# Six Strassen blocks in two runs of three instead of seven in one run, one weight sum of each made a block ahead by an adding DMA

## The chip, the cores and the metric

The kernel runs on one core of a Trainium2 chip. The metric is the device time of one execution in microseconds. Before the change it is 1360.77 us, the median of three runs (1360.38 to 1362.2). A core has five engines with a queue of their own: TensorE (PE) does matrix products, VectorE (DVE) and ScalarE (ACT) work on tiles in on-chip memory, GpSimd (POOL) does small work and issues the DMAs that add while they write, SyncE (SP) issues most plain DMAs. Each engine takes its instructions in program order and waits on semaphores.

## The reference

Two layers on a sequence of 512 tokens of width 1024. Layer 0 mixes by retention and neighbourhood attention, layer 1 by a state space scan. After each mixer stands the same channel mixer, in which most of the change lies:

```python
def conv_geglu_ffn(hn, w_up, conv_w, conv_b, w_down):
    u = depthwise_conv_centered(hn @ w_up, conv_w, conv_b)
    gate, val = jnp.split(u, 2, axis=-1)
    return (jax.nn.gelu(gate, approximate=True) * val) @ w_down
```

`w_up` has 2 x 2816 columns: 22 feature blocks of 128 columns for the gate and 22 for the value, f = 0 to 21.

## The kernel before

**Products.** Every float32 product is made of three TensorE products in a faster format: an operand x is split into a high part (a cast on ACT, L115) and a low part (x minus the high part, on DVE, L116), and `mm3` adds high by high, low by high and high by low (L125, L126, L127). So every 128 x 1024 weight tile costs ACT one cast and DVE one subtraction before TensorE can use it. The split weights go into a ring of four places (`weight`), each free again when TensorE has used it; the loaded tiles before that stand in a pool of three (`wst`).

**Up-projection.** `ffn` takes the blocks f one after another. A plain block needs 24 products of 512 columns for the gate and 24 for the value, then its `tail`: the convolution (three instructions for each of gate and value, two of them on DVE), gelu, and the product into `H[:, f]`.

**Strassen blocks.** For f in `UP` the pair f, f + 1, gate and value together, is one 2 x 2 block product by Winograd's form of Strassen's rule: seven products in place of eight, each of 24 matmuls of 256 columns, 168 matmuls in all (`up_strassen`). The combinations of the activations are made once (`combos`). Those of the weights are made in each block by `weights(i)` just before product i: four tiles are loaded, q11, q12, q22 and q21 (`w_up[s, f + h]`); DVE makes q12 + q22, then q0 = q11 + (q12 + q22), later q0 + q21 (three additions, L469); and one more sum, q11 + `w_up[1, f]`, is made by a DMA that adds (L484, issued by POOL). The seven tiles are split like any others. DVE also adds three of the results into G and V, and the `tail`s of the pair are done during the next block (`held`). With `UP = (6, 8, 10, 12, 14, 16, 18)` seven such blocks follow each other without a break; f = 20, 21 are plain again.

**Tiles that stay.** q11, q12 and so on live in the three `wst` tiles and two `gain` tiles that `E.held` keeps for a whole run of blocks; block number `nth` takes them by `(2 * nth + j) % 3`.

**Order.** The program is written in order of dependence; the scheduler of the recording layer then puts each engine's instructions in order by priority, and an instruction of low priority whose inputs are ready may move forward. `weights(i)` stands in `tc.high_priority(60)`. The first step of the down-projection's preparation, `A21 = A11 - A21` over H[:, :11] (L329 in `raw`), moves forward this way as soon as the blocks f = 0 to 10 are done: it then stands on DVE inside a Strassen block. `E.in_turn` orders the instructions of a block after the last split and load.

**Chores.** The down-projection also uses combinations of its weights. They are sums in DRAM, 32 DMAs of 704 KB a layer issued by POOL (L293 in `sums`): 16 copies and 16 that add. `E.chore()` issues the next one, after the last product that has been recorded. They are called in the mixer of the same layer (a "c" in the strings `PAIRS` and `SLOTS` that order the steps of a head pair or group), after plain blocks, and twice in each Strassen block (i = 1 and 4).

**State space layer.** `SLOTS` has one string for each of four groups: h = one head (its rows `pb` are loaded by ACT's queue, three buffers ahead), i and p = parts of a pair's output, n = a projection of the next group, o = an output projection, c = a chore.

Of the kernel before, what the change touches and what calls it, by code (L numbers as in the profile page):

```python
# [8 lines left out]
F32 = mybir.dt.float32  # L9
# [4 lines left out]
ALU = mybir.AluOpType  # L14
# [3 lines left out]
P = 128  # L18
# [382 lines left out]
    E.late += [lambda s=s: E.finish(s, st, done) for s in LATE]  # L401


UP = (6, 8, 10, 12, 14, 16, 18)


def combos(E, pool, raw):
# [38 lines left out]
def up_strassen(E, pool, w_up, f, X, G, V, held):  # L446

    nc, tc = E.nc, E.tc  # L450
    low, high = slice(0, HW), slice(HW, S)

    nth = UP.index(f)
    if f - 2 not in UP:
        E.held = [[E.wst.tile([P, 1024], F32, name="wst") for _ in range(3)],
                  [E.gain.tile([P, D], F32, name="gain") for _ in range(2)]]
    (st12, st11), (st0, st21) = [E.held[0][(2 * nth + j) % 3] for j in range(2)], E.held[1]

    def load(st, s, h):
        E.load = nc.sync.dma_start(st, w_up[s, f + h])  # L460
        return st

    def parts(st, i):
        hi, lo = E.weight(SKEW if i else 0)
        E.split(hi, lo, st)
        E.last = E.pair + (E.load,)
        return hi, lo

    add = lambda o, x, y: nc.vector.tensor_tensor(o, x, y, op=ALU.add)  # L469
    q = {}  # L470

    def weights(i):
        with tc.high_priority(60), E.in_turn():
            if i == 0:
                q[11] = load(st11, 0, 0)
                return parts(q[11], i)
            if i == 1:
                q[12] = load(st12, 1, 0)
                with E.in_turn(E.load):
                    q[22] = load(pool.tile([P, 1024], F32, name="wu", tag=f"e{nth % 2}"), 1, 1)  # L480
                add(q[12], q[12], q[22])
                q[0] = st0
                add(q[0], q[11], q[12])
                nc.gpsimd.dma_start(q[11], w_up[1, f], accum_op=ALU.add, max_dma_last_dim=4096)  # L484
                return parts(q[12], i)
            if i == 2:
                return parts(q[0], i)
            if i == 3:
                q[21] = load(st21, 0, 1)
                add(q[0], q[0], q[21])  # L490
                return parts(q[0], i)
            return parts(q[{4: 11, 5: 21, 6: 22}[i]], i)

    a = E.mm.tile([P, S], F32, name="mm")
    b, d = (E.px.tile([P, S], F32, name="pu", tag="px") for _ in range(2))
    order = ("A11", a), ("S3", b), ("S2", a), ("A22", b), ("R1", a), ("A12", d), ("S4", a)
    for i, (n, bank) in enumerate(order):
        hi, lo = weights(i)
        more = i in (2, 3, 4, 6)
        r = bank.rearrange("p (j c) -> p j c", j=2)  # L500
        for j in range(2):
            for k in range(4):
                c = slice(j * 512 + k * P, j * 512 + k * P + P)
                E.mm3(r[:, j], hi[:, c], lo[:, c], X[n][0][:, k], X[n][1][:, k], not more and j + k == 0, k == 3, more or j > 0)
        if i in (3, 5):
            o = G[:, :, low if i == 3 else high]
            add(o, r, o)
        elif i == 4:
            t = E.tmp.tile([P, 2, HW], F32, name="w5", tag="tmp")
            nc.scalar.copy(t, r)  # L510
            add(V[:, :, low], t, V[:, :, low])
        else:
            nc.scalar.copy({0: G[:, :, high], 1: V[:, :, low], 2: G[:, :, low], 6: V[:, :, high]}[i], r)
        if i in (1, 4):
            E.chore()
        if i in (3, 5) and held:
            held.pop(0)()


def ffn(E, w_up, cw, w_down, ts, g_post_row, done, w1=None):  # L520
# [3 lines left out]
    with ExitStack() as ctx:  # L524
# [44 lines left out]
        for f in range(2, NF):  # L569
            if f in UP or f - 1 in UP:  # L570
                if f in UP:
                    G, V = (cp.tile([P, 2, S], F32, name=n, tag=t) for n, t in
                            ((("G", "k0"), ("V", "k1")) if UP.index(f) % 2 else (("G", "k2"), ("V", "k3"))))
                    up_strassen(E, hp, w_up, f, X, G, V, held)
                    held.extend(partial(tail, f + j, G[:, j], V[:, j], True) for j in range(2))
                    while held and f + 2 not in UP:
                        held.pop(0)()
                continue
            ps = []
            for s in range(2):  # L580
                behind = w1 and f == 2
                with E.in_turn() if f > UP[0] else nullcontext():
                    st = E.wload(w_up[s, f], E.mid if behind and s == 0 else None)
                    w = E.wunit(None, st=st, behind=E.turned[3][1] if behind else None)
                E.last = E.pair + (E.load,)
                ps.append(E.mm.tile([P, S], F32, name="mm"))
                E.proj_fm(ps[-1], w)
            tail(f, *ps)
            E.chore(1 + (f == 2))
            if f < UP[0]:  # L590
                X = next(make)
            if f == NF - 2:
                big = hp.tile([P, 32, HW], R32, name="big")
                for k in range(0, HK, 4):
                    c = slice(k, min(k + 4, HK))
                    E.split(big[:, c], big[:, HK + k:HK + c.stop], H[:, c, HW:])
# [40 lines left out]
def mixer0(E, w0, w_v, w_fm, tabs, dist_d, logit, gn, bias, w_out, g_post_row, done):  # L637
# [286 lines left out]

SLOTS = (
# [4 lines left out]
)  # L930

# [563 lines left out]
```

## Time and profile before

| What | Value |
| --- | --- |
| Time, median of three runs | 1360.77 us |
| Time of the profiled execution | 1356.96 us |
| Span of the profiled execution | 1355.2 us |
| TensorE busy | 1325.2 us (98%) |
| VectorE busy | 1124.9 us (83%) |
| ScalarE busy | 841.6 us (62%) |
| Seven Strassen blocks, layer 0 | 340.61 to 481.85 us |
| Seven Strassen blocks, layer 1 | 1083.43 to 1221.81 us |
| Groups 1 and 2 of the state space layer | about 774 to 923 us |

The profile names an instruction by engine, source line, operation and tiles (`out<-in`). A busy TensorE says little here, since the end of a matmul is modelled and overlaps the next one's start: the distance from one start to the next is its pace. A number in brackets at the end of a timeline row is the engine's idle time before that instruction and who ended it.

### The profile page before, as it was taken

The numbers are of one execution on the slowest core, as the hardware profiler recorded it, in microseconds if no ns is written. First come the engines' busy times: TensorE is split into PE (matmuls) and PEld (weight loads), VectorE is DVE, ScalarE is ACT, GpSimd is POOL, SyncE is SP. The second block draws the span as 40 slices with busy tenths as digits, with TensorE's granted clock in tenths as the row PEclk, the third lists the DMA queues.
The fourth block names the chain that finished last, engine by engine and source line by source line (L and its number), as shares of the span: only waits on it lengthen the run. The fifth ranks groups of instructions, "written<-read, shape, count | busy, mean of one in ns | idle before, by whom it ended". The sixth has DMA issues, their size and how long they took to land.

```text
span 1355.2 us, 20474 instructions
## 1 busy us (share of the span) xinstructions
PE 1325.2 (98%) x7784; PEld 1139.2 (84%) x7784; DVE 1124.9 (83%) x1554; ACT 841.6 (62%) x1353; POOL 125.5 (9%) x144
## 2 busy tenths in 40 slices
PE   7999999999999999999999999999999999999998
PEld 6877777898999988888778788787879899998886
DVE  7368888696799998797878876798789789999886
ACT  5356667453565766664878878477545467666663
POOL 1011111101110000020000110011011111110001
PEclk9999999999999999999999999999999999999999
DMA  8454447348983545564466475285544789684654
GB/s 294 146 208 161 159 135 217 103 123 197 217 206 100 151 143 194 190 210 129 138 181 195 126 247 185 90 250 162 183 133 152 203 197 220 166 225 146 193 183 148
DMA packets 71393, 237.28 MB, mean 175 GB/s; under 512 B 8576, under 2 KB 9344, under 8 KB 70784
## 3 DMA queue, kind: packets, MB, share of 16 engines
q1 hardware_dynamic: 54224, 167.30, 36.8%
q0 software_dynamic: 9184, 53.48, 17.6%
q10 hardware_dynamic: 7888, 15.21, 4.2%
q8 instruction: 61, 1.00, 0.3%
q14 instruction: 36, 0.29, 0.1%
HBM read 228.35 MB, written 51.64 MB: 207 GB/s over the span
## 4 chain that ended last, share of the span: by engine, by line
PE 77%; DVE 10%; ACT 5%; DMA 4%; issue 3%; SPq 1%; POOL 0%; DVEq 0%; POOLq 0%; ACTq 0%
PE mm L125 20%; PE mm L127 20%; PE mm L126 20%; DVE ring L116 3%; PE pu L126 2%; PE pu L125 2%; PE pu L127 2%; DMA pb<-pd 1%; PE pi L1155 1%; PE st L1104 1%; ACT pb L1134 1%; PE py L1175 1%; DVE cv L533 1%; DMA wst<-in_c_fm 1%; PE pt L182 1%
## 5 line engine op out<-in xcount | busy, mean ns | idle before, releaser
L125 PE MATMUL mm<-xh,ring 128*128 128x512 f32 (+1 forms) x880 | 321.0, 365 | 1.3 <-ACT z L1074 0.9
L116 DVE TENSOR_TENSOR ring<-wst,ring 128x1024 fp32r<-128x1024 f32 (+1 forms) x218 | 265.4, 1222 | 67.4 <-ACT ring L115 67.2
L127 PE MATMUL mm<-xl,ring 128*128 128x512 f32 (+2 forms) x880 | 320.0, 364 | 1.1 <-DVE mean L958 0.6
L126 PE MATMUL mm<-xh,ring 128*128 128x512 f32 (+2 forms) x880 | 319.8, 364 | 1.1 <-DVE ring L116 1.1
L115 ACT CAST ring<-wst 128x1024 fp32r<-128x1024 f32 (+1 forms) x218 | 224.4, 1034 | 122.3 <-PE mm L126 64.0
L125 PEld LDWEIGHTS mm<-xh,ring 128*128 128x128 f32 x880 | 165.4, 188 | 29.3 <-issue 2.7
L127 PEld LDWEIGHTS mm<-xl,ring 128*128 128x128 f32 (+1 forms) x880 | 165.1, 188 | 28.1 <-issue 1.1
L126 PEld LDWEIGHTS mm<-xh,ring 128*128 128x128 f32 (+1 forms) x880 | 165.4, 188 | 27.0 <-DVE ring L116 1.7
L125 PE MATMUL mm<-xc,ring 128*128 128x256 f32 x336 | 93.1, 277 | 0.0
L127 PE MATMUL mm<-xc,ring 128*128 128x256 f32 x336 | 93.1, 277 | 0.0
L126 PE MATMUL mm<-xc,ring 128*128 128x256 f32 x336 | 93.1, 277 | 0.0
L1134 ACT ACTIVATE pb<-pb,tok 128x128 f32<-128x128 f32 x256 | 80.7, 394 | 10.0 <-DMA pb<-pd 8.9
L125 PE MATMUL mm<-ring,big 128*128 128x512 f32 x164 | 64.0, 390 | 0.0
L127 PE MATMUL mm<-ring,big 128*128 128x512 f32 x164 | 63.8, 389 | 0.0
L126 PE MATMUL mm<-ring,big 128*128 128x512 f32 x164 | 63.8, 389 | 0.0
L127 PEld LDWEIGHTS mm<-xc,ring 128*128 128x128 f32 x336 | 63.1, 188 | 0.0
L125 PEld LDWEIGHTS mm<-xc,ring 128*128 128x128 f32 x336 | 63.1, 188 | 0.0
L126 PEld LDWEIGHTS mm<-xc,ring 128*128 128x128 f32 x336 | 63.0, 188 | 0.0
L125 PE MATMUL pu<-xh,ring 128*128 128x256 f32 x224 | 62.5, 279 | 0.1
L126 PE MATMUL pu<-xh,ring 128*128 128x256 f32 x224 | 62.3, 278 | 0.1
L127 PE MATMUL pu<-xl,ring 128*128 128x256 f32 x224 | 62.1, 277 | 0.0
L293 POOL DMA_DIRECT2D ts<-in_f_down x48 | 31.0, 652 | 280.3 <-PE mm L127 229.5
(360 smaller groups left out, 3120.8 us busy)
## 6 DMA issues: line engine op xcount, KB each, us to landing
ts<-in_f_down POOLq DMA_DIRECT2D x48, 704.0 KB, 6.3
wst<-in_f_up SPq DMA_DIRECT2D x60, 512.0 KB
wst<-in_c_fm SPq DMA_DIRECT2D x40, 512.0 KB
wst<-ts SPq DMA_DIRECT2D x32, 512.0 KB
pb<-pd ACTq DMA_DIRECT2D x29, 512.0 KB
wst<-in_f_down SPq DMA_DIRECT2D x24, 512.0 KB
ts<-ts POOLq DMA_DIRECT2D x16, 704.0 KB, 7.2
wst<-in_ab_fm SPq DMA_DIRECT2D x20, 512.0 KB
```

What stands on the lines that cost most here:

```text
L115: first = self.nc.scalar.copy(hi, src)
L116: second = self.nc.vector.tensor_tensor(lo, src, hi.bitcast(F32), op=ALU.subtract)
L125: mm(out, lh, rh, start=first, stop=False)
L126: mm(out, ll, rh, start=False, stop=False)
L127: self.product = mm(out, lh, rl, start=False, stop=last)
L182: last = nc.tensor.transpose(pt[:, j], xs[:, j * P:(j + 1) * P], self.ident)
L293: out.append(lambda i=i, src=src, j=j, c=c, kw=kw: gp.dma_start(part(ts, i, c), part(src, j, c), **kw))
L533: nc.vector.scalar_tensor_tensor(o[:, :S - 1], ps[:, 1:], w(2), o[:, :S - 1], op0=ALU.mult, op1=ALU.add)
L1104: nc.tensor.matmul(ps, o["bt"][:, c], xs, start=True, stop=True)
L1134: nc.scalar.activation(pb[:, dr, c], pb[:, dr, c], AF.Identity, scale=1.0 - 2 * dr, bias=tok[:, 0, c, dr * H + h:dr * H + h + 1])
L1155: nc.tensor.matmul(pi[:, c - 1 + dr], o["st"][dr, i][:, q * P:(q + 1) * P], o["t"][1][:, c * C:(c + 1) * C], start=True, stop=True)
L1175: E.together([nc.tensor.matmul(py[j * 64:j * 64 + 64, c * C:(c + 1) * C], o["x"][:, c, (2 * q + j) * 64:(2 * q + j + 1) * 64], ms[j][0][:, c],
```

## The change

- `UP` loses 12: f = 12 and 13 become plain blocks, so the Strassen blocks stand in two runs of three, f = 6, 8, 10 and f = 14, 16, 18.
- In the first block of a run all is as before. In the second and third, q12 + q22 is no longer made by DVE: during product 2 of the block before, SP loads the next block's q12 into the third kept tile (`ahead`) and POOL issues a DMA that adds q22 to it (`onto`). q22 itself, which the last product needs, is loaded at product 3 of its own block.
- Every load of a run is ordered after the load before it (`in_turn(E.load)`).
- `E.chore()` is called once in a Strassen block (i = 4) instead of twice.
- `SLOTS` gets four more "c": two in the string of group 1, two in that of group 2.

```diff
-UP = (6, 8, 10, 12, 14, 16, 18)
+UP = (6, 8, 10, 14, 16, 18)
...
-    (st12, st11), (st0, st21) = [E.held[0][(2 * nth + j) % 3] for j in range(2)], E.held[1]
-
-    def load(st, s, h):
-        E.load = nc.sync.dma_start(st, w_up[s, f + h])
+    first, more_blocks = f - 2 not in UP, f + 2 in UP
+    (st12, st11, ahead), (st0, st21) = [E.held[0][(2 * nth + j) % 3] for j in range(3)], E.held[1]
+
+    def load(st, s, h, f=f):
+        with E.in_turn(E.load):
+            E.load = nc.sync.dma_start(st, w_up[s, f + h])
         return st
+
+    def onto(st, f, h):
+        nc.gpsimd.dma_start(st, w_up[1, f + h], accum_op=ALU.add, max_dma_last_dim=4096)
+
+    def load22():
+        q[22] = load(pool.tile([P, 1024], F32, name="wu", tag=f"e{nth % 2}"), 1, 1)
...
             if i == 1:
-                q[12] = load(st12, 1, 0)
-                with E.in_turn(E.load):
-                    q[22] = load(pool.tile([P, 1024], F32, name="wu", tag=f"e{nth % 2}"), 1, 1)
-                add(q[12], q[12], q[22])
+                q[12] = st12
+                if first:
+                    load(st12, 1, 0)
+                    load22()
+                    add(st12, st12, q[22])
                 q[0] = st0
                 add(q[0], q[11], q[12])
-                nc.gpsimd.dma_start(q[11], w_up[1, f], accum_op=ALU.add, max_dma_last_dim=4096)
+                onto(q[11], f, 0)
                 return parts(q[12], i)
             if i == 2:
+                if more_blocks:
+                    load(ahead, 1, 0, f + 2)
+                    onto(ahead, f + 2, 1)
                 return parts(q[0], i)
             if i == 3:
                 q[21] = load(st21, 0, 1)
+                if not first:
+                    load22()
                 add(q[0], q[0], q[21])
...
-        if i in (1, 4):
+        if i == 4:
             E.chore()
...
-    "s0 G R s1 s2 h0 i0 i1 o0 c h1 h2 o1 c p0 h4 h3 p1 h5 i2 n0 c n1 p2 n6 c n3 h6 n7 n2 n9 N i3 n8 h7 p3 n4 n5 N",
-    "G R s0 s1 o0 c h2 o1 c s2 h0 h1 i1 i0 p0 h3 p1 h4 i2 n0 c h5 N n1 n3 c p2 n2 n4 i3 h6 h7 p3 n5 N",
+    "s0 G R s1 s2 h0 i0 i1 o0 c h1 h2 o1 c p0 h4 h3 p1 h5 i2 n0 c n1 p2 n6 c n3 h6 n7 n2 c n9 N i3 n8 c h7 p3 n4 n5 N",
+    "G R s0 s1 o0 c h2 o1 c s2 h0 h1 i1 i0 p0 h3 p1 h4 i2 n0 c h5 N n1 n3 c p2 n2 c n4 c i3 h6 h7 p3 n5 N",
```

On TensorE the program differs in one place a layer only: the 168 matmuls of 256 columns of one block become 96 of 512 columns. On DVE and ACT it is the same outside the two stages that hold the Strassen blocks.

**On DVE, in the second block of layer 0** (f = 8; its weights are prepared while the first block's last products run). `wst_3104` is q11, `wst_3106` is q12, `wu_3348` is q22, `gain_3107` is q0. Before:

```order
L469 TENSOR_TENSOR G_3102<-pu_3110,G_3102 128x2x256
L116 TENSOR_TENSOR ring_69<-wst_3104,ring_69 128x1024
L469 TENSOR_TENSOR wst_3106<-wst_3106,wu_3348 128x1024
L469 TENSOR_TENSOR gain_3107<-wst_3104,wst_3106 128x1024
L469 TENSOR_TENSOR V_3103<-w5_3256,V_3103 128x2x256
L116 TENSOR_TENSOR ring_69<-wst_3106,ring_69 128x1024
```

and with the change:

```order
L477 TENSOR_TENSOR G_3102<-pu_3110,G_3102 128x2x256
L116 TENSOR_TENSOR ring_69<-wst_3104,ring_69 128x1024
L477 TENSOR_TENSOR gain_3107<-wst_3104,wst_3106 128x1024
L477 TENSOR_TENSOR V_3103<-w5_3257,V_3103 128x2x256
L116 TENSOR_TENSOR ring_69<-wst_3106,ring_69 128x1024
```

The addition of q22 has gone from DVE; nothing else has moved here.

**On DVE, the early step of the down-projection** (L329) in layer 0. Before, it stands in the fourth block, behind the addition of product 3 into G, and ahead of the addition into V, the split of the next block's q11 and its q12 + q22:

```order
L116 TENSOR_TENSOR ring_69<-wu_3802,ring_69 128x1024
L469 TENSOR_TENSOR G_3768<-pu_3771,G_3768 128x2x256
L329 TENSOR_TENSOR H_2534<-H_2534 128x11x256
L469 TENSOR_TENSOR V_3769<-w5_3926,V_3769 128x2x256
L116 TENSOR_TENSOR ring_69<-wst_3104,ring_69 128x1024
L469 TENSOR_TENSOR wst_3106<-wst_3106,wu_4027 128x1024
```

With the change it stands where the first block of the second run (f = 14) is prepared, between the addition of q21 and the split of that sum for product 3, among the tails of the plain block f = 13:

```order
L116 TENSOR_TENSOR ring_69<-gain_3928,ring_69 128x1024
L547 SCALAR_TENSOR_TENSOR cv0_3912<-mm_3858,cwt_2558,cv0_3912 128x511
L477 TENSOR_TENSOR gain_3928<-gain_3928,gain_3929 128x1024
L329 TENSOR_TENSOR H_2534<-H_2534 128x11x256
L546 SCALAR_TENSOR_TENSOR cv1_3917<-mm_3887,cwt_2558,cv1_3917 128x511
L116 TENSOR_TENSOR ring_69<-gain_3928,ring_69 128x1024
```

The three instructions that stood behind it (the addition into V, the split of q11, q12 + q22 of the next block) now have no 128 x 11 x 256 step ahead of them.

**On POOL, group 1 of the state space layer.** `sq` is the sum of squares of a pair's output, `rg` the root for a group, a DMA into `ts` is a chore. Before:

```order
L1218 TENSOR_TENSOR rg<-ss,head 128x4
L293 DMA ts_221<-in_f_down 16x11264 x2
L1187 TENSOR_TENSOR sq<-sq 128x512
L293 DMA ts_221<-in_f_down 16x11264
L1187 TENSOR_TENSOR sq<-sq 128x512
L293 DMA ts_221<-in_f_down 16x11264
L1187 TENSOR_TENSOR sq<-sq 128x512
```

and with the change:

```order
L1232 TENSOR_TENSOR rg<-ss,head 128x4
L293 DMA ts_221<-in_f_down 16x11264 x2
L1201 TENSOR_TENSOR sq<-sq 128x512
L293 DMA ts_221<-in_f_down 16x11264
L1201 TENSOR_TENSOR sq<-sq 128x512
L293 DMA ts_221<-in_f_down 16x11264 x3
L1201 TENSOR_TENSOR sq<-sq 128x512
```

Two chores have joined the fourth of the group, ahead of the last pair's sum of squares: one issued after projection n2, one after n8.

## The prediction

> **What bounds the kernel now.** I read the page first: the busy time of the engines, then the shares of the chain that ended last.
>
> ```profile
> PE 1325.2 (98%) x7784; PEld 1139.2 (84%) x7784; DVE 1124.9 (83%) x1554; ACT 841.6 (62%) x1353; POOL 125.5 (9%) x144
> PE 77%; DVE 10%; ACT 5%; DMA 4%; issue 3%; SPq 1%; POOL 0%; DVEq 0%; POOLq 0%; ACTq 0%
> ```
>
> TensorE ends the kernel, and 98% is an average. The tenth of the chain that DVE holds must lie in places. So next came the table by windows, with one window for each Strassen block (from its first matmul to the next block's). Its columns are the window, its length, busy time and count on PE, PEld, DVE, ACT and POOL, granted clock, DMA share and GB/s; layer 0 first, then four of layer 1's seven blocks.
>
> ```profile
> 340.61:359.81 19.20, 19.20 (x170) 19.19 (x168) 14.37 (x15) 10.89 (x13) 3.54 (x4) 1.00 0.81 181
> 359.81:379.01 19.20, 19.20 (x171) 19.20 (x169) 16.78 (x20) 13.78 (x18) 2.69 (x3) 1.00 0.90 214
> 379.01:398.21 19.20, 19.20 (x171) 19.20 (x169) 18.04 (x22) 12.04 (x16) 2.41 (x3) 1.00 0.86 210
> 398.21:417.84 19.63, 19.57 (x170) 19.37 (x169) 19.49 (x21) 12.10 (x17) 0.28 (x1) 1.00 0.52 146
> 417.84:442.30 24.46, 22.10 (x170) 21.55 (x169) 23.15 (x28) 15.20 (x20) 0.87 (x1) 0.93 0.37 109
> 442.30:462.20 19.90, 19.90 (x170) 19.90 (x169) 19.90 (x24) 13.59 (x18) 0.86 (x1) 1.00 0.51 159
> 462.20:481.85 19.65, 19.65 (x171) 19.65 (x170) 19.65 (x26) 14.99 (x20) 0.89 (x1) 1.00 0.53 161
> ```
>
> ```profile
> 1083.43:1102.62 19.19, 19.19 (x169) 19.18 (x168) 14.36 (x15) 10.90 (x13) 3.52 (x4) 1.00 0.82 179
> ...
> 1160.22:1182.68 22.46, 20.37 (x170) 19.97 (x169) 22.46 (x27) 15.28 (x20) 2.68 (x3) 1.00 0.73 187
> 1182.68:1202.59 19.91, 19.89 (x171) 19.70 (x170) 19.91 (x24) 13.59 (x18) 2.68 (x3) 1.00 0.90 227
> 1202.59:1221.81 19.22, 19.22 (x171) 19.22 (x169) 19.22 (x25) 14.56 (x20) 1.82 (x2) 1.00 0.72 184
> ```
>
> An undisturbed block takes 19.20 us. DVE starts a run with room (14.37 busy), fills block by block, and from the fourth on is busy all the time: it needs slightly more per block than TensorE. What is lost is small but for one block in each layer, 24.46 and 22.46. The timelines of DVE and PE show why:
>
> ```profile
> 413.41 3.08 DVE L329 TENSOR_TENSOR H<-H 128x2816 f32<-128x2816 f32 x1
> ...
> 1155.20 3.08 DVE L329 TENSOR_TENSOR H<-H 128x2816 f32<-128x2816 f32 x1
> ```
>
> ```profile
> 423.61 0.39 PE L126 MATMUL pu<-xc,ring 128*128 128x256 f32 x1 [2.20 <-DVE ring L116]
> ...
> 426.09 0.41 PE L125 MATMUL pu<-xc,ring 128*128 128x256 f32 x1
> 426.30 0.41 PE L126 MATMUL pu<-xc,ring 128*128 128x256 f32 x1
> ...
> 1165.40 0.39 PE L126 MATMUL pu<-xc,ring 128*128 128x256 f32 x1 [2.02 <-DVE ring L116]
> ```
>
> L329 puts 3.08 us on a DVE without room; ten microseconds later TensorE waits 2.20 and 2.02 us for a split. In layer 0 it then runs a stretch at 0.21 us a matmul (426.09 to 426.30), about half speed, and the clock of that window is 0.93; in layer 1 it is 1.00.
>
> **Part 1: one Strassen block becomes two plain blocks.** A plain block's pace is the distance between two chores, each issued when a plain block's last product has ended:
>
> ```profile
> 319.42 0.85 POOL L293 DMA_DIRECT2D ts<-in_f_down  x1 [9.10 <-PE mm L127]
> ...
> 341.18 0.90 POOL L293 DMA_DIRECT2D ts<-ts  x1 [9.07 <-PE mm L127]
> ```
>
> One such row lies between them, so a pair takes 341.18 − 319.42 = 21.76 us. The rule saves only 21.76 − 19.20 = 2.56 us a block, less than the disturbed blocks lost. A layer without losses would take 6 × 19.20 + 21.76 = 136.96. Before, layer 0 takes 481.85 − 340.61 = 141.24 and layer 1 takes 1221.81 − 1083.43 = 138.38. So the change is worth **−4.28** and **−1.42, together −5.70**, if every loss goes.
>
> [...]
>
> **Part 2: does every loss go?** Each sum taken from DVE is one of these:
>
> ```profile
> L469 DVE TENSOR_TENSOR wst<-wst,wu 128x1024 f32<-128x1024 f32 x14 | 17.1, 1219 | 0.0
> ```
>
> 1.22 us, in four blocks a layer. Blocks four, six and seven of layer 0 ran over by 0.43, 0.70 and 0.45 with DVE full; 1.22 is more than each. And a run is now three blocks long, while the first three blocks lost nothing even with that sum. Between the runs, DVE has in 21.76 us two tails (four steps of about 0.75 and one of 0.68 each, 7.4), four splits (4.9) and four tiles of the next block (4.9), an estimated 17.2. So the second run begins with room again.
>
> L329 now falls to the first block of the second run. There the first rows above show DVE's idle time in such a block: 19.20 − 14.37 = 4.83 us, more than 3.08. The addition of q21 stands ahead of it; the split for product 3 and a tail stand behind it. I cost it at nothing; if that cover is gone, it costs what it did, the two disturbed blocks.
>
> **Part 3: the sum by DMA.** DVE's q0 = q11 + (q12 + q22) now waits for a plain load and an adding DMA on the third kept tile, which is free once the block before has split it (345.25 for f = 10). What is queued behind that DVE instruction is the addition into V and the split for product 1.
>
> ```profile
> 345.25 1.23 DVE L116 TENSOR_TENSOR ring<-wst,ring 128x1024 fp32r<-128x1024 f32 x1 [0.36 <-ACT ring L115]
> ...
> 374.53 1.23 DVE L469 TENSOR_TENSOR gain<-wst 128x1024 f32<-128x1024 f32 x1
> ```
>
> ```profile
> wst<-in_f_up POOLq DMA_DIRECT2D x14, 512.0 KB, 7.0
> ```
>
> An adding DMA takes 7.0 us. For the load in front I take 6.54, the time of a `pb` load of the same size (quoted below). 345.25 + 6.54 + 7.0 = 358.8, and doubling both gives 372.3, still ahead of 374.53 − 1.22. So nothing; between 0 and 1.5 us (a fifth of 7.0 late, an estimate) for each of 8 blocks at the worst. SP and POOL issue early and wait for little else here; traffic is about as before, since one chore (704 KB) goes where one adding DMA (512 KB) comes. Nor does the missing chore give anything: the blocks with the highest DMA share (0.90) ran in 19.20.
>
> **Part 4: four chores in the state space layer.** A chore elsewhere in that layer shows its size, in the DMA view from 894 to 900 us:
>
> ```profile
> q0 software_dynamic: 32, 0.72, 31.6%
> ```
>
> 31.6% of 6 us, so 1.9 us of all sixteen DMA engines. The chore after n8 is issued when that product ends. The chain of waits there:
>
> ```profile
> 836.40 0.25 PE mm L127
> ...
> 839.70 6.54 DMA pb<-pd
> 846.24 0.02 issue
> 846.26 2.75 ACT pb L1134 x9
> ...
> 854.13 0.76 DVE xf L1068
> 854.89 0.14 issue
> 855.02 0.47 PE mm L125
> ```
>
> From 836.65 (n8's end) the chore's packets come just ahead of, or among, those of a `pb` load that is already late: ACT waits for it, then DVE, then TensorE. What is put ahead of it passes through to TensorE: **+2.0 us** (an estimate of 1.9, rounded up for its issue). The transfers around it, 836 to 848 us:
>
> ```profile
> q1 hardware_dynamic: 583, 1.60, 48.4%
> q10 hardware_dynamic: 544, 1.05, 23.2%
> ```
>
> The load's own packets, two loads of 512 KB in q10, need 0.232 × 12 / 2 = 1.39 us each, and the load took 6.54: it stood behind others. [...]
>
> The chore after n2 is issued when that product ends, just before this row:
>
> ```profile
> 822.60 0.78 ACT L1065 ACTIVATE xf<-mm,cwt 128x512 f32<-128x512 f32 x1 [0.22 <-PE mm L127]
> ```
>
> ACT has little slack there (0.22), but no load that it waits for; 14 us ahead of the late one I give it 0. Those of group 2 (after n2 and n4, estimated at 909 and 915 from the order of the products) lie before this gap of ACT:
>
> ```profile
> 923.09 0.78 ACT L1065 ACTIVATE xf<-mm,cwt 128x512 f32<-128x512 f32 x1 [3.27 <-PE mm L127]
> ```
>
> 3.27 us of slack cover 1.9 each, so 0. The bounds of the four are 0 and 4 × 2.0 = 8; below nothing I see no way, since they add traffic and remove none here.
>
> **Sum:** −5.70 + 2.0 = −3.7. The profiled execution took 1356.96 with a span of 1355.2: 1353.3 and 1351.5 after. The timed median stands 3.8 above it; the difference carries over: 1360.77 − 3.7 = **1357.1 us**.
>
> **Rivals.**
> - *All chores hidden:* if the `pb` loads keep their turn: −5.7, 1355.1. For it, the DMA share has gaps; against, the 6.54 above.
> - *Two or more chores late:* n2's, or one of group 2, costs 2.0 too: 1359.1; with all four 1363.1. For it, ACT waits in this layer are on the chain; against, the 3.27.
> - *L329's stall only moves* (the other side): if it comes when the first block's splits have no room, both losses stay, 24.46 − 19.20 = 5.26 and 22.46 − 19.20 = 3.26, 8.5 together: −5.7 + 2.0 + 8.5 = +4.8, **1365.6**. It decides when less than 3.08 us of the 4.83 is left ahead of the split for product 3.
> - *The adding DMA is late:* 1.5 us in 8 blocks, 12 in all: 1357.1 + 12 = 1369. It decides when load and addition together take twice what they took; block three at a DMA share of 0.86 speaks against it.
> - *The change doesn't relieve DVE where it matters:* if the small losses of the late blocks come from ACT or the ring, some 2 stay: 1359.1. Against it, DVE is full there and ACT is at 12 to 15 of 19 us.
>
> **How the numbers follow.** Forecast 0.42, all hidden 0.22, two or more chores late 0.16, L329 0.08, adding DMA 0.04, no relief 0.08. About 0.2%, 2.7 us, is what a measurement of this kernel can tell from none: 1358.05 to 1363.5 is the same. Of the forecast nine tenths are faster; all hidden is faster; chores late and no relief are the same; L329's 1365.6 is slower in six of ten; the adding DMA is slower. Faster 0.38 + 0.22 = 0.60, same 0.04 + 0.16 + 0.08 + 0.03 = 0.31, slower 0.05 + 0.04 = 0.09. The range goes from just below all hidden, 1354.6, over two chores late and no relief to three late, 1361.2; outside are the two slow rivals and four late chores, under 2 in 10.
>
> **What will show it.** Right: six blocks a layer of 19.20 each, the pair f = 12, 13 at 21.8, clock 1.00 in all of them; no PE idle time of over a microsecond behind the two L329s; q0's addition on DVE without idle time before it. In group 1, ACT's wait for `pb` near 846 grown by about 2 us, and PE's at 855 with it. Wrong: PE idle with DVE's L116 as releaser behind L329, DVE waiting for `wst<-in_f_up` from POOL, a group 2 stretched by more than 1 us, or blocks still at 19.6 to 19.9.

## The result, and the profile after

The changed kernel takes **1368.27 us** (median of 12 runs), the kernel before, run beside it, 1359.31 (12 runs): ratio **1.0069**, 95% interval 1.0048 to 1.009. It is slower, where 1357.1 was forecast. The profiled execution took 1368.22 us with a span of 1366.4, against 1356.96 and 1355.2 before, so it shows 11.2 us to be found. By stage, from the first matmul of 256 columns of a layer's Strassen blocks to the start of the matmul that follows their last:

| Stage, us | Before | After | Difference |
| --- | --- | --- | --- |
| Strassen stage, layer 0 | 141.24 | 145.86 | +4.62 |
| Between the two stages (state space layer included) | 601.58 | 604.88 | +3.30 |
| Strassen stage, layer 1 | 138.38 | 141.67 | +3.29 |
| All else | 473.98 | 474.03 | +0.05 |

The table by windows of the changed kernel, layer 0: three blocks, the plain pair, three blocks (window, length, busy time and count on PE, PEld, DVE, ACT and POOL, clock, DMA share, GB/s).

```profile
340.33:359.53 19.20, 19.20 (x170) 19.19 (x168) 13.74 (x15) 10.78 (x13) 3.62 (x4) 1.00 0.96 203
359.53:380.93 21.40, 19.89 (x170) 19.70 (x169) 16.65 (x20) 13.70 (x18) 1.84 (x2) 1.00 0.64 160
380.93:404.55 23.62, 21.41 (x170) 21.22 (x169) 18.12 (x22) 13.55 (x18) 0.91 (x1) 0.93 0.51 120
404.55:426.32 21.77, 21.77 (x98) 18.02 (x97) 21.69 (x28) 11.14 (x15) 2.65 (x3) 1.00 0.82 203
426.32:445.51 19.19, 19.19 (x169) 19.19 (x168) 16.08 (x16) 10.79 (x13) 3.58 (x4) 1.00 0.95 212
445.51:466.99 21.48, 19.89 (x170) 19.70 (x169) 16.66 (x20) 13.70 (x18) 0.86 (x1) 1.00 0.60 157
466.99:486.19 19.20, 19.20 (x171) 19.20 (x169) 17.77 (x22) 13.68 (x18) 0.00 (x0) 1.00 0.44 142
```

The plain pair takes what was forecast, and the block with L329 (426.32) loses nothing. But the second block of each run and the third of the first lose 2.2 to 4.4 us, where the second and third block of the layer lost nothing before, and DVE is about as busy there as it was (16.65 and 18.12 us against 16.78 and 18.04). In the block that loses 4.4 us a part goes with the clock of its window, 0.93. The groups of instructions name a wait that the kernel before did not have:

```profile
L125 PE MATMUL pu<-xh,ring 128*128 128x256 f32 x192 | 54.7, 285 | 7.6 <-ACT V L527 7.6
```

TensorE waits at product 3 for L527, ACT's copy of product 1's result, which frees the bank that product 3 writes to. The timelines of ACT, of PE and of POOL in the second block:

```profile
362.67 0.57 ACT L527 COPY G<-mm 128x512 f32<-128x512 f32 x1
367.93 1.04 ACT L115 CAST ring<-wst 128x1024 fp32r<-128x1024 f32 x1 [4.69 <-DMA wst<-in_f_up]
368.88 0.58 ACT L527 COPY V<-pu 128x512 f32<-128x512 f32 x1
```

```profile
369.52 0.39 PE L125 MATMUL pu<-xh,ring 128*128 128x256 f32 x1 [1.51 <-ACT V L527]
```

```profile
351.53 0.90 POOL L466 DMA_DIRECT2D wst<-in_f_up  x1 [9.73 <-DMA wst<-in_f_up]
354.66 0.92 POOL L293 DMA_DIRECT2D ts<-ts  x1 [2.23 <-PE mm L127]
355.67 0.91 POOL L466 DMA_DIRECT2D wst<-in_f_up  x1
```

The copy stands behind a cast on ACT, and the cast waits for the *old* adding DMA, which makes q11 + `w_up[1, f]` for product 4. POOL issues the new one (351.53), the chore (354.66) and the old one (355.67) within 4.1 us. The DMA view gives the old one's time from issue to landing, 12.2 us:

```profile
wst<-in_f_up POOLq DMA_DIRECT2D x1, 512.0 KB, 12.2
```

Before, POOL had only the chore ahead of it, and further ahead. POOL's timeline of the kernel before, and its DMA view:

```profile
354.96 0.88 POOL L293 DMA_DIRECT2D ts<-ts  x1 [7.33 <-PE mm L127]
357.16 0.91 POOL L484 DMA_DIRECT2D wst<-in_f_up  x1 [1.32 <-DVE V L469]
```

```profile
wst<-in_f_up POOLq DMA_DIRECT2D x1, 512.0 KB, 8.4
```

So it landed at 357.16 + 8.4 = 365.6, 5.8 us into its block (359.81). With the change it landed at 367.9, 8.4 us into the block (359.53). Product 3 begins 8.3 us into an undisturbed block (2.88 for the first product and 2 × 2.72 for the next two, by the starts of the matmuls) and went on 369.52 − 367.9 = 1.6 us after the landing, so the latest harmless landing is about 6.7 us into the block. The margin had been 0.9 us; in the third block, where the old one was issued at 376.41, took 8.9 and so landed 6.3 us in, it had been 0.4.

The third block of the changed kernel, which loses most, has no new DMA ahead of its old one, since a run's last block prepares no next one. POOL's timeline and the DMA view of the old one there:

```profile
375.85 0.90 POOL L293 DMA_DIRECT2D ts<-ts  x1 [19.27 <-PE mm L127]
376.76 0.94 POOL L466 DMA_DIRECT2D wst<-in_f_up  x1
```

```profile
wst<-in_f_up POOLq DMA_DIRECT2D x1, 512.0 KB, 12.7
```

So a chore 0.9 us ahead is enough to make the old one late; the last section has all the places side by side.

(The chain of waits of this execution breaks off after a tenth of the span, so the waits are read from groups and timelines.)

### The profile page after: what moved, and what is told of

Read it like the earlier page. It is cut to its first block, busy times and chain, and to the rows that moved or that the text cites. A ratio compares the mean times of both kernels' runs of the same rounds, so it can differ in the third digit from the quotient of the medians.

```text
span 1366.4 us, 20157 instructions
## 1 busy us (share of the span) xinstructions
PE 1329.9 (97%) x7640; PEld 1135.9 (83%) x7640; DVE 1101.6 (81%) x1528; ACT 830.2 (61%) x1337; POOL 130.0 (10%) x150
## 5 line engine op out<-in xcount | busy, mean ns | idle before, releaser
L125 PE MATMUL mm<-xh,ring 128*128 128x512 f32 (+2 forms) x928 | 341.4, 368 | 2.1 <-ACT z L1088 1.7
L127 PE MATMUL mm<-xl,ring 128*128 128x512 f32 (+2 forms) x928 | 340.4, 367 | 1.1 <-DVE mean L972 0.6
L116 DVE TENSOR_TENSOR ring<-wst,ring 128x1024 fp32r<-128x1024 f32 (+1 forms) x220 | 267.7, 1223 | 91.2 <-ACT ring L115 90.9
L126 PE MATMUL mm<-xh,ring 128*128 128x512 f32 (+2 forms) x928 | 340.2, 367 | 1.0 <-DVE ring L116 1.0
L125 PEld LDWEIGHTS mm<-xh,ring 128*128 128x128 f32 (+1 forms) x928 | 174.4, 188 | 32.5 <-issue 2.7
L127 PEld LDWEIGHTS mm<-xl,ring 128*128 128x128 f32 (+1 forms) x928 | 174.0, 188 | 30.7 <-issue 1.1
L126 PEld LDWEIGHTS mm<-xh,ring 128*128 128x128 f32 (+1 forms) x928 | 174.4, 188 | 29.0 <-DVE ring L116 1.4
L125 PE MATMUL mm<-xc,ring 128*128 128x256 f32 x288 | 80.0, 278 | 0.0
L126 PE MATMUL mm<-xc,ring 128*128 128x256 f32 x288 | 79.9, 277 | 0.0
L127 PE MATMUL mm<-xc,ring 128*128 128x256 f32 x288 | 79.8, 277 | 0.0
L545 ACT ACTIVATE cv<-mm,cwt 128x512 f32<-128x512 f32 x40 | 31.1, 777 | 60.4 <-PE mm L127 60.4
L125 PE MATMUL pu<-xh,ring 128*128 128x256 f32 x192 | 54.7, 285 | 7.6 <-ACT V L527 7.6
L125 PEld LDWEIGHTS mm<-xc,ring 128*128 128x128 f32 x288 | 54.2, 188 | 0.0
L127 PEld LDWEIGHTS mm<-xc,ring 128*128 128x128 f32 x288 | 54.2, 188 | 0.0
L126 PEld LDWEIGHTS mm<-xc,ring 128*128 128x128 f32 x288 | 54.1, 188 | 0.0
L127 PE MATMUL pu<-xl,ring 128*128 128x256 f32 x192 | 54.0, 281 | 0.0
```

The costliest lines, as they stand in the source:

```text
L116: second = self.nc.vector.tensor_tensor(lo, src, hi.bitcast(F32), op=ALU.subtract)
L125: mm(out, lh, rh, start=first, stop=False)
L126: mm(out, ll, rh, start=False, stop=False)
L127: self.product = mm(out, lh, rl, start=False, stop=last)
L545: nc.scalar.activation(o, ps, AF.Identity, scale=w(1), bias=w(3))
```

## The experiments

Eleven kernels; each ratio is against the kernel before on the same chip. "Stages" are the two Strassen stages, "between" the time between them, of one profiled execution each. The time between scatters by some us from one execution to the next (604.88 to 609.60 over the changed kernel and the first three of the table, whose edits all lie inside the Strassen blocks), so it serves for large differences only.

| Kernel | Median us | Ratio (95% interval) | Stages us | Between us |
| --- | --- | --- | --- | --- |
| Change, chore after product 1 | 1356.32 | 0.9976 (0.9958 to 0.9994) | 136.97, 141.16 | 609.60 |
| Change, chore after product 5 | 1356.61 | 0.9992 (0.9983 to 1.0001) | 136.97, 136.97 | 609.57 |
| Change, q12 + q22 on DVE | 1356.42 | 0.9976 (0.9962 to 0.999) | 136.97, 136.98 | 604.95 |
| Before, two runs of three | 1353.31 | 0.9958 (0.9943 to 0.9973) | 136.98, 136.98 | 603.50 |
| Before, L329 later | 1352.05 | 0.9962 (0.9944 to 0.9979) | 137.56, 136.75 | 600.50 |
| Before, all four chores | 1362.69 | 1.0025 (1.0008 to 1.0042) | 140.85, 138.76 | 605.61 |
| Before, chore after n8 | 1363.78 | 1.0036 (1.0017 to 1.0056) | 139.44, 140.14 | 610.39 |
| Before, three other chores | 1358.78 | 1.0007 (0.9989 to 1.0026) | 139.62, 139.00 | 601.49 |
| Change, both costs taken out | 1355.50 | 0.9963 (0.9944 to 0.9982) | 136.97, 136.97 | 604.11 |
| Seven blocks, L329 later, new DMA | 1351.17 | 0.9926 (0.9898 to 0.9954) | 136.48, 136.85 | 602.22 |
| The same, extra chore in the last block | **1347.77** | **0.9922** (0.9905 to 0.9938) | 134.39, 134.39 | 604.36 |

### What makes the old adding DMA late

First, the chore out of its way:

```diff
-        if i == 4:
+        if i == 1:
             E.chore()
```

> The changed kernel with one edit: the chore of a Strassen block is called after product 1 instead of product 4. In the changed kernel the chore is issued about 1 us ahead of the DMA that adds w_up[1, f] to q11, and that DMA takes 11 to 12.7 us where it took 5.2 to 8.9 before; ACT's cast waits for it, the copy of product 1 (L527) stands behind the cast, and TensorE waits 0.4 to 2.4 us for that copy. Theory A, crowding (chore, new adding DMA and weight loads all fall in the same half of a block): with the chore moved, q11's DMA takes under 9 us, TensorE's waits on L527 are all gone, each Strassen stage falls from 145.9 and 141.7 us to 137 to 138.5, and the time is 10 to 12 us below the changed kernel, about 1357. Rival B, the new adding DMA alone (wherever the chore stands): the waits stay above 1 us in the second block of each run and go only in the third; stages 141 to 143, about 3 us below the changed kernel, 1365.

12 us below the changed kernel, as theory A has it. Layer 0's stage is 136.97; of the waits on L527 one was left in layer 1 (f = 16, 2.0 us) in the profiled execution, which took 1363.58, seven above the median. POOL's timeline there has the chore gone, but the new DMA directly ahead of the old (one row for both):

```profile
1184.39 1.80 POOL L466 DMA_DIRECT2D wst<-in_f_up  x2 [10.98 <-DMA wst<-in_f_up]
```

Rival B falls as a rule, since the new DMA is ahead of the old one in all four second blocks and one of them was late. In that one the new DMA delays the old one mostly by holding up its issue: it waits on POOL for its own load to land, and the old one, behind it in POOL's order, was issued 0.5 us ahead of its block instead of 3.3 to 3.9 in the three others. Once issued it took 9.3 us, against 8.7 to 8.8 in those.

Then the chore kept, and the new adding DMA taken away:

```diff
-                if first:
-                    load(st12, 1, 0)
-                    load22()
-                    add(st12, st12, q[22])
+                load(st12, 1, 0)
+                load22()
+                add(st12, st12, q[22])
...
-                if more_blocks:
-                    load(ahead, 1, 0, f + 2)
-                    onto(ahead, f + 2, 1)
...
-                if not first:
-                    load22()
```

> The changed kernel with q12 + q22 made by DVE in every block as before (no load and no adding DMA a block ahead, q22 loaded at product 1); two runs of three, one chore a block after product 4 and the four chores in the state space layer stay. Theory A (crowding by the new adding DMA and the moved loads): q11's DMA takes 8 to 9 us, no wait on L527, stages 137 to 138.5 us as DVE has room in runs of three, time about 1357, 10 to 12 below the changed kernel. Rival B (the new adding DMA alone) says the same. Rival C, the place of the chore right ahead of q11's DMA: the waits on L527 stay in the second and third block of a run at 0.4 us or more, stages 140 or more. Rival D, DVE without room: waits on the split L116 of over 1 us in each run, stages 140 or more.

All four runs of blocks at 19.20; the old DMA, issued at 359.01, took 8.5 us in the second block. Rival D falls. Rival C falls as it was put, but this kernel differs in two things at once: the new DMA is gone, and with its sum back on DVE the old one is issued later, 2.3 us behind the chore (356.75) instead of 1.0. The third block of the changed kernel tells the two apart: there the chore alone, 0.9 us ahead, made it 12.7 us. So it is the chore right ahead that makes the old DMA late, and its nearness counts; that the new DMA is needed for it isn't shown. That leaves order against bandwidth: the chore stays beside the old DMA, but behind it.

```diff
-        if i == 4:
+        if i == 5:
             E.chore()
```

> The changed kernel with the chore of a Strassen block called after product 5: it is then issued some 1 to 2 us behind the DMA that adds to q11, not ahead of it, but still beside its packets and in the same half of the block. Theory A1, order in POOL's queue (the packets ahead of q11's DMA delay it, those behind don't): q11's DMA takes under 9.5 us, waits on L527 gone, Strassen stages 137 to 138.5, time about 1356 to 1357 as with the chore after product 1. Rival A2, bandwidth alone (all packets in that half share the DMA engines, whatever the order): q11's DMA still takes over 10 us and waits on L527 of 0.4 to 2 us stay, stages over 140, time 1361 or more.

POOL's timeline of this kernel, and its DMA view for the second of these:

```profile
351.69 0.90 POOL L466 DMA_DIRECT2D wst<-in_f_up  x1 [9.66 <-DMA wst<-in_f_up]
355.90 0.89 POOL L466 DMA_DIRECT2D wst<-in_f_up  x1 [3.31 <-DVE V L477]
357.61 0.90 POOL L293 DMA_DIRECT2D ts<-ts  x1 [0.83 <-PE pu L127]
```

```profile
wst<-in_f_up POOLq DMA_DIRECT2D x1, 512.0 KB, 5.5
```

12.2 us became 5.5, with the same DMAs in the same half of the block, and every block takes 19.20. In the three other second blocks the old DMA took 7.9 to 8.3, in the third blocks 5.4 to 5.5. **A1 holds against A2: a chore issued 1 us ahead makes the old DMA late, one issued 1.7 us behind does not.** Order alone doesn't say why a chore 1.0 us ahead costs so much more than one 2.2 us ahead (12.2 against 8.4, while the chore itself takes 9.9 us to land instead of 7.1); that stays open.

### What the room on DVE is worth

The first part of the change alone, on the kernel before:

```diff
-UP = (6, 8, 10, 12, 14, 16, 18)
+UP = (6, 8, 10, 14, 16, 18)
```

> The kernel before with UP = (6, 8, 10, 14, 16, 18) and nothing else: DVE sums, two chores a block, no more chores in the state space layer. If the room of DVE in runs of three is what matters, both Strassen stages take 137 to 138.5 us (before 141.2 and 138.4), L329 costs no TensorE wait, and the time is 3 to 5.7 us below the kernel before. Rival, L329's stall only moves: a wait of about 2 us on L116 in f = 14 or 16 stays in each layer, stages 139 or more, and the time within 2 us of the kernel before.

136.98 and 136.98, against 136.96 in the prediction's sum; the ratio is worth 0.0042 × 1359 = 5.7 us (3.7 to 7.7), where −5.70 stood. The rival falls: no wait on L116 is left. This kernel is below both of the case's kernels, with q12 + q22 still made by DVE in every Strassen block: in runs of three, DVE had room for it.

Was a block worth giving up? Here seven blocks stay and only L329 moves:

```diff
         if i == 1:
-            tt(A21, A11, A21, op=ALU.subtract)
+            with E.in_turn():
+                tt(A21, A11, A21, op=ALU.subtract)
```

> The kernel before with seven blocks in one run, and L329 (3.08 us on DVE) ordered behind the last split of the plain block f = 21, so that it stands in no Strassen block. If L329 on a full DVE was what the fifth blocks lost, they take 19.2 to 19.9 instead of 24.5 and 22.5, the stages 135.5 to 137 us each, and the time is 4 to 7 us below the kernel before, as with two runs of three, though no block was given up. Rival, DVE's deficit itself: each block from the fourth on is still short of DVE time, the shortage adds up and a wait of over 1 us appears in the sixth or seventh block; stages 137.5 or more, or the 3 us come back as a wait of TensorE at the start of the down-projection.

The same gain from one line. The fifth blocks fall from 24.46 and 22.46 to 20.09 and 19.76. Layer 1's stage is as expected and layer 0's half a microsecond above, as its late blocks still lose. No wait of a microsecond is left in the blocks, and the 3 us don't come back behind them: between the stages it takes 600.5 us against 601.6, and outside them 474.3 against 474.0. The windows of the last four, layer 0:

```profile
398.20:417.88 19.68, 19.68 (x171) 19.68 (x169) 19.51 (x23) 13.54 (x19) 0.55 (x2) 1.00 0.49 144
417.88:437.97 20.09, 19.88 (x170) 19.68 (x169) 19.92 (x24) 13.55 (x19) 0.83 (x2) 1.00 0.44 131
437.97:457.75 19.78, 19.78 (x170) 19.59 (x169) 19.61 (x24) 13.24 (x19) 0.55 (x2) 1.00 0.53 161
457.75:478.17 20.42, 20.11 (x171) 19.91 (x169) 20.28 (x26) 15.02 (x21) 0.71 (x1) 1.00 0.54 155
```

### What the four chores cost

All four on the kernel before, then n8's alone, then the three others (the strings `SLOTS` differ in the "c"s only):

> The kernel before with the strings SLOTS of the changed kernel and nothing else: four more chores in groups 1 and 2 of the state space layer, four fewer at the end of layer 1's up-projection. The trace of the changed kernel has 3.3 us more between the two Strassen stages than before, 2.7 of them at two waits for DVE's xf in group 1 (after 855 us, 1.8 and 1.9 where one of 1.0 stood). Theory: the chore after n8 holds back the pb load; group 1 grows by 2 to 3 us, group 2 by less than 0.5, the time by 2 to 3. Rival: the growth belongs to where the state space layer happens to start, or to chance; then within 0.5 us of the kernel before.

> The kernel before with one more chore in the state space layer, that after projection n8 in group 1. All four together cost 3.4 us (1.0025) in the run before. Theory (the prediction's step): n8's chore is the only one that is late: it holds the pb load issued near 840 us back to 9 to 10 us and costs the whole 2 to 3.4. Rival: n2's chore costs a part too (with all four a wait of 1.5 us for xf stood near 828, which the kernel before has at 0.3): then n8's alone costs 1.5 to 2.3.

> The kernel before with the three other chores (after n2 in group 1, after n2 and n4 in group 2). Theory (the prediction's step): within 0.5 us of the kernel before, no longer wait for pb or xf near 828 us. Rival: n2's chore holds back the pb load issued 1.5 us ahead of it (6.9 us with all four), a wait of 1 to 1.5 us for xf appears near 828, and the time is 1 to 2 us above the kernel before; group 2 unchanged within 0.5 in both.

All four cost 0.0025 × 1359 = 3.4 us (1.1 to 5.7), n8's alone 4.9 (2.3 to 7.6), the three others within the measurement of nothing. The chain of waits shows the `pb` load that was named, with n8's chore alone and then with the three others:

```profile
840.10 10.24 DMA pb<-pd
```

```profile
838.14 6.69 DMA pb<-pd
```

6.54 before, 10.24 with n8's chore, 6.69 with the others: it is n8's. The rival put the wait for xf near 828 us down to n2's chore, but the kernel with n8's alone, which has no chore after n2, waits 1.8 us there, and the one with the three others 0.8. What lengthens those (0.2 to 3.3 us over the executions) stays open.

### Both costs out, and the parts that hold put together

```diff
-        if i == 4:
+        if i == 5 or i == 1 and f == UP[0]:
             E.chore()
...
-n7 n2 c n9 N i3 n8 c h7 p3 n4 n5 N
+n7 n2 c n9 N i3 n8 h7 p3 n4 n5 N
```

> The changed kernel with its two costs taken out: the chore of a Strassen block after product 5 (two in the first block), and no chore after n8; two runs of three and the adding DMA a block ahead stay. If these two were all that the change lost, stages of 137.0 and the state space layer as before: 1353 to 1355, the same as two runs of three alone (1353.3), so the adding DMA itself brings nothing there. Rival: a further cost of the change is left, 1357 or more.

0.9963 and stages of 136.97, as two runs of three alone (0.9958): within these intervals nothing else was lost, and in runs of three the new adding DMA brings nothing.

In a run of seven it should. There: `UP` as before, L329 later, the new DMA, the chore after product 5, a second chore in the first two blocks, none after n8.

> The parts that proved good, together: seven Strassen blocks in one run as before, L329 ordered behind the split of f = 21, q12 + q22 by the adding DMA a block ahead as in the change, the chore of a block after product 5 (two in the first two blocks), three more chores in the state space layer, not the one after n8. With the order in POOL's queue mended and DVE relieved by 1.13 us in each of six blocks a layer, all blocks should take 19.2 to 19.4: stages 134.4 to 135.5 (137.6 and 136.8 with L329 later alone), time 1347 to 1350. Rival: DVE was not what the late blocks of a seven-block run lost (ACT's queue or q11's DMA was), then stages 136.5 or more and 1352 as without the adding DMA.

Part of it came. The late blocks all took 19.19 to 19.20, so DVE was what they lacked. But the second block of layer 0 took 21.3, the second of layer 1 19.8 and the third 21.1, with the wait on L527 again. POOL's timeline shows why:

```profile
346.71 0.85 POOL L293 DMA_DIRECT2D ts<-ts  x1 [4.71 <-PE pu L127]
357.14 1.80 POOL L467 DMA_DIRECT2D wst<-in_f_up  x2 [9.57 <-DMA wst<-in_f_up]
358.42 1.43 POOL L293 DMA_DIRECT2D ts<-ts  x1
```

The second chore went first, and the new DMA came only just ahead of the old (both in the row x2), which was then issued 1.9 us ahead of its block instead of 3.9 and took 10.2 us. What the new DMA waited for is its own load, issued at 348.83, behind that chore. In the kernel with both costs taken out the same second chore stood 0.3 us behind that load (346.96 against 346.68), the new DMA was issued at 352.05, and nothing was lost; so a second chore there does not always do harm. Here it was moved to the last block, which issues no DMA ahead:

```diff
-        if i == 5 or i == 1 and f in UP[:2]:
+        if i == 5 or i == 1 and f == UP[-1]:
```

> The run before this one (seven blocks, L329 later, adding DMA a block ahead, chore behind product 5) with the second chore of the first two blocks moved to the last block, where no DMA a block ahead is issued. In the run before, that second chore pushed the DMA a block ahead to within a microsecond of q11's, which then took 10.2 and 10.7 us; TensorE waited 1.6 and 1.3 us for the copy L527 there, while all blocks behind them took 19.2. If the order on POOL's queue is the whole cause, every block takes 19.2, both stages 134.4, and the time falls by 2 to 4 us to 1347 to 1349 (ratio 0.990 to 0.992). Rival: the late waits come from the start of a seven-block run whatever the chores: stages stay at 136 or more, ratio 0.9925.

All fourteen blocks take 19.20, both stages 134.39. The ratios of this kernel and the one before it, 0.9922 and 0.9926, are too near to rank them; the stages differ by 4.6 us in the profiles. The windows of its last four blocks, to lay beside those with L329 later alone:

```profile
398.90:418.10 19.20, 19.20 (x170) 19.20 (x169) 18.78 (x23) 13.78 (x19) 2.68 (x3) 1.00 0.82 198
418.10:437.30 19.20, 19.20 (x170) 19.20 (x169) 18.79 (x23) 13.78 (x19) 2.68 (x3) 1.00 0.83 208
437.30:456.50 19.20, 19.20 (x170) 19.20 (x169) 18.80 (x23) 13.79 (x19) 1.81 (x2) 1.00 0.66 176
456.50:475.70 19.20, 19.20 (x170) 19.20 (x169) 17.97 (x23) 13.87 (x19) 0.00 (x0) 1.00 0.64 183
```

DVE's busy time falls below 19.2, and the loss with it. **This kernel beats both: 10.6 us below the kernel before** (0.0078 × 1359; 8.4 to 12.9).

## Why the prediction was wrong

**Parts 1 and 2 held.** The plain pair at 21.77, blocks of 19.20 in runs of three, and L329 without cost in the second run: the first part alone gave the 5.7 us forecast (3.7 to 7.7). That it came out to the decimal is luck, since a part of the 4.28 for layer 0 belonged to the profiled execution (last section). The rival "L329's stall only moves" fell, and so did "doesn't relieve DVE". One size in Part 2 was off without harm: DVE was busy for 21.69 of the 21.77 us of the pair, not for 17.2, since the tails of the last Strassen block fall there too; the room that covered L329 was that of the first block behind it (16.08 busy of 19.19).

**Part 3 failed**, at "So nothing" and at "SP and POOL issue early and wait for little else here; traffic is about as before". It asked whether the *new* DMA lands in time, and that answer was right (7.5 us after 351.53, while DVE adds q0 of f = 10 at 374.9). It did not ask who stands behind it on POOL's queue. That is the old adding DMA. Without DVE's sum it was issued 1.2 us sooner (3.9 us ahead of its block, at 355.67 for 359.53, against 2.7, at 357.16 for 359.81), and so the chore stood 1.0 instead of 2.2 us ahead of it: it took 10.4 to 12.7 us in the seven blocks where that was so, and in the second blocks the new DMA stood ahead as well. The cost was set at 0; it is (145.86 + 141.67) − 2 × 136.96 = 13.6 us in the profile, a part of it the clock of one block, 0.93. Against the kernel with the chore after product 5 it is 1368.3 − 1356.6 = 11.7 in the medians and (1.0069 − 0.9992) × 1359 = 10.5 by the ratios. The rival "the adding DMA is late", at 1369 and with a chance of 0.04, has the right kind and by chance the right size, but its wait was put at DVE's q0 and its condition on the new DMA.

The number was in the trace of before: the old DMA landed 5.8 us into the second block and 6.3 into the third, and was needed at about 6.7. One row was misread there: of the two blocks with a DMA share of 0.90, layer 0's ran in 19.20, but layer 1's in 19.91.

**Part 4 had the right mechanism, the wrong size.** The term was 2.0, from the chore's own 1.9 us of DMA time. The `pb` load was held back 10.24 − 6.54 = 3.7 us, and the time by 3.4 (all four) to 4.9 (n8's alone), two intervals that overlap. Why 3.7 and not 1.9 no run shows.

**The sum** by measured terms: −5.7 (blocks and room) + 11.7 (old adding DMA) + 3.4 (chores) = +9.4, and 0.0069 × 1359 = 9.4 (6.5 to 12.2). The match to the decimal is chance: with the 10.5 by the ratios it is +8.2, and each term has an interval of some us.

## What to carry to other kernels

Where a change puts a DMA on a queue, or lets one be issued sooner, work out the landing of every DMA behind it and how close each follows the one ahead, and lay the landing beside the time at which its reader's engine needs it, with what stands behind that reader; a DMA that can wait goes behind the one that can't (here 5.5 us to landing instead of 12.2). Before work is given up to relieve an engine, look for the single movable instruction that fills it: here one line (L329) was worth as much as the broken run of blocks. An idea that loses in one arrangement can win in another: the adding DMA brought nothing in runs of three and mended the late blocks of a run of seven, once the queue was in order.

## What the runs showed of the hardware

The same idle time did not always go with a slower clock. Four executions had a wait of 2.20 us behind L329 in layer 0. The windows of that block with all four chores, and with the three others:

```profile
417.86:442.00 24.14, 21.94 (x170) 21.55 (x169) 22.83 (x28) 15.21 (x20) 0.86 (x1) 0.93 0.36 110
```

```profile
417.72:440.05 22.33, 20.05 (x171) 19.60 (x169) 22.33 (x28) 14.89 (x20) 0.86 (x1) 1.00 0.39 119
```

In two executions (24.46 and 24.14 us) the clock was 0.93, in two (22.74 and 22.33) 1.00. Nor did the shorter wait always leave it alone: with n8's chore alone, a wait of 1.96 us in layer 1's fifth block went with a clock of 0.93 and 23.81 us, where the kernel before had 2.02, 1.00 and 22.46. What decides it no run shows. So a part of the 4.28 us forecast for layer 0 belonged to the profiled execution, not to the kernel.

The time of an adding DMA of 512 KB, from issue to landing, went by what POOL had issued shortly ahead of it. These are the old ones of the second and later blocks of a run:

| Ahead of it | Us to landing | Kernel |
| --- | --- | --- |
| Nothing for 6 us | 5.2 to 5.7 | Before |
| The new adding DMA, 4.2 to 4.5 us ahead (a chore 1.7 behind) | 5.5 to 8.3 | Change, chore after product 5 |
| A chore, 3.2 to 4.2 us ahead | 6.7 to 7.3 | Before |
| A chore, 2.1 to 2.3 us ahead | 7.8 to 8.9 | Before |
| A chore, 2.2 to 2.3 us ahead | 7.6 to 8.9 | Change, q12 + q22 on DVE |
| A chore, 0.9 to 1.0 us ahead | 10.4 to 12.7 | Change, third blocks with a chore |
| A chore, 1.0 us ahead, and the new adding DMA 2.9 to 4.5 | 11.0 to 12.3 | Change, second blocks |
